# Reordering a normalisation and a rotary turn, and running seven more blocks by a seven-product scheme, in a hybrid encoder layer

## The chip, the cores and the metric

The kernel runs on one core of a Trainium2 chip. The metric is device time in microseconds (us) of one execution. The engines named below are TensorE (PE, matrix products into PSUM, 8 banks), VectorE (DVE), ScalarE (ACT), GpSimd (POOL), and the queues that issue DMAs (SP's, ACT's and POOL's).

## What is computed

One encoder layer for 256 tokens of width 2048, all in float32. Three mixers read the same normed tokens: multi-head latent attention (8 heads, rotary key shared), a gated short convolution, and cross-attention of 4 heads into 256 memory tokens. Three sigmoid gates weigh their projections; then comes an output projection, a convolutional SwiGLU feed-forward block (width 5632) and a last norm.

```python
h = rmsnorm(x, mix_norm)
z = h @ w_in        # [q latent 512 | kv latent 512 | rotary key 64 | conv 3 x 1024 | memory query 1024 | 3 gates x 2048]
q  = (rmsnorm(c_q, q_norm) @ w_uq).reshape(B, S, 8, 128 + 64)     # the last 64 are turned by the rotary angles
kv = (rmsnorm(c_kv, kv_norm) @ w_ukv).reshape(B, S, 8, 128 + 128)
y_mla  = mla_attention(q_nope, q_rope, k_nope, apply_rope(k_r, cos, sin), v) @ w_o_mla
y_conv = (cb * dwconv_centred(cc * cv, conv_w)) @ w_out_conv
y_mem  = memory_attention(q_x, rmsnorm(mem, mem_norm), w_mem_kv) @ w_o_mem
gates  = sigmoid(g + gate_bias)
x = x + (gates[0] * y_mla + gates[1] * y_conv + gates[2] * y_mem) @ w_o
u = dwconv_centred(rmsnorm(x, ffn_norm) @ w_up, ffn_conv_w); a, b = split(u, 2)
x = x + (silu(a) * b) @ w_down
return rmsnorm(x, final_norm)
```

## The kernel before

**Number format.** Every float32 operand is split into a high and a low half, `hi` (a copy by ACT, L146) and `lo` (a difference by DVE, L147), and a product is made of three matmuls (hi·hi, lo·hi, hi·lo). Activations lie side by side as `[hi | lo]` in one tile, 256 + 256 columns. A weight block is 128 x 2048 numbers, 1 MB: SP's queue loads it into one of 3 `raw` buffers, ACT and DVE split it into one of 3 `hi` and one of 3 `lo` buffers, and PE uses it for some 5.5 us.

**Pools.** Activations of 512 columns lie in one pool, `slots`, of 54 buffers: normed tokens `xs` (16), memory tokens `ms` (16), memory keys `kx` (8) and values `vx` (8), latents, memory queries `qx` (8), heads' probabilities and results, gates, and later the feed-forward's tiles. Work tiles of 512 columns (biases, `t`, `sums`) lie in a tag of 4 buffers. Matmul results go to 5 PSUM banks (`mmps`), attention and transposes to 3 (`atps`).

**Order.** The program is written as one straight list; loops are unrolled. When it is built, a scheduler places each engine's instructions in a fixed order, by the place in the program and by when it reckons that operands and buffers are to be had. On the chip every engine works through its list in order and waits on semaphores.

**Stages.** (1) Latents of keys and values, then of queries (not yet normed: `kvz`, `qz`); memory keys; token norms; memory values. (2) L422 to L427: each of the 8 latent tiles is multiplied by its factor `fb` and split into a new slot (`zkv`, `zq`). (3) L430 to L450: the positions are loaded and brought into range on DVE in a chain of some 20 small steps, and ACT makes `sin` and `cos` in the slot `rot`. (4) The rotary key (L559 to L568), then 8 memory query tiles (L572 to L588), each one block of `w_in`, its total (`total`: ACT copies one half of the bank, DVE adds the other) and its split into a slot `qx`. At tile 0 the rotary key is folded, its halves are swapped by four small DMAs (`swapped`), turned (`rope`) and split (`krs`). At every odd tile a memory head is begun; `advance` carries each head in flight by one step: scores and softmax (`p`), transposes (`ph`, `pl`), products with the values (`om`). (5) Convolution blocks alternate with the steps in `STEPS`: rotary queries `r` (four matmul groups, totals into two slots `qr`), keys, values, queries, latent heads 0 to 7. (6) Six gate runs (class `Two`), one for each branch and half of the columns; after each run `gated` makes the sigmoids and two projections follow. (7) Output projection, then twice: 22 `up` steps and the down runs (`Two` again, three in all), with `added` adding their eight products to the residual.

**The seven-product scheme.** A `Two` run multiplies 256 tokens by 1024 columns over 8 (gates) or 11 (down) blocks, each of two 128-row parts. It works on 2 x 2 quarters. `plain` makes 8 quarter products, 24 matmuls of 512 columns. `fast` makes 7, 21 matmuls, but of sums: of the weights (L786 to L788, and a second split, L781 and L782) and of the tokens (`token_sums`, L724 to L736, into two slots `sh`, `sl`). The eight results of a run (`q1` to `q7` and `d`) take all 8 PSUM banks. `GATES` and `FAST` name the blocks that are fast: 6 x 3 in the gate runs and 3 x 4 in the down runs, 30 in all. The gates' token sums are made ahead of all gate runs (`hsums`, L838 to L844), the down runs' within `up`.

Of the kernel before, what the change touches and what calls it, by code (L numbers as in the profile page):

```python
# [11 lines left out]
F32 = mybir.dt.float32  # L12
# [3 lines left out]
ALU = mybir.AluOpType  # L16
# [47 lines left out]
WAKE = 6  # L64
NW = D // 512
KEPT = 10
GATES = (1, 3, 5)
FAST = (1, 3, 5, 7)
STEPS = "r - k0 v0 - q0 0 1 2 3 k1 v1 q1 4 5 - 6 - 7 -"
STEP = 4096.0  # L70
COARSE = _parts(TWO_PI * STEP, 7, 5)
# [7 lines left out]
def tile_kernel(ctx: ExitStack, tc: tile.TileContext, a, out):  # L79
# [3 lines left out]
    raws = ctx.enter_context(tc.tile_pool(name="raws", bufs=3))  # L83
    his = ctx.enter_context(tc.tile_pool(name="his", bufs=3))
    los = ctx.enter_context(tc.tile_pool(name="los", bufs=3))
    slots = ctx.enter_context(tc.tile_pool(name="slots", bufs=54))
    tmp = ctx.enter_context(tc.tile_pool(name="tmp", bufs=2))
    tiny = ctx.enter_context(tc.tile_pool(name="tiny", bufs=2))
    mmps = ctx.enter_context(tc.tile_pool(name="mmps", bufs=5, space=PSUM))
# [5 lines left out]
    def slot(name, dtype=F32):  # L95
        return slots.tile([P, 2 * T], dtype, tag="slot", name=name)

    def half(t, i):
        return t[:, i * T : (i + 1) * T]
# [16 lines left out]
    def col(name, i=0):  # L116
        if name == "fcw":
            return taps[:, i : i + 1]
        c = COLS[name] + i
        return cols[:, c : c + 1]  # L120
# [82 lines left out]
    def split(dst, src, gain=None):  # L203

        w = dst.shape[1] // 2
        if gain is None:
            nc.scalar.activation(dst[:, 0:w], src, AF.Copy)
            nc.vector.tensor_tensor(dst[:, w:], src, f32(dst[:, 0:w]), op=ALU.subtract)
        else:
            nc.scalar.activation(dst[:, 0:w], src, AF.Copy, scale=gain)  # L210
            nc.vector.scalar_tensor_tensor(
                dst[:, w:], src, gain, f32(dst[:, 0:w]), op0=ALU.mult, op1=ALU.subtract
            )
# [23 lines left out]
    def spread(r, dst=None):  # L237

        ps = atps.tile([P, 2 * T], F32, tag="at", name="pss")
        for h in range(2):  # L240
            dg = tmp.tile([P, P], F32, tag="dg", name="dg")
            nc.vector.tensor_scalar(dg, ident, r[:, h : h + 1], None, op0=ALU.mult)
            nc.tensor.matmul(ps[:, h * P : (h + 1) * P], ones, dg, start=True, stop=True)
        if dst is None:
            return ps[:, 0:T]
        nc.scalar.activation(dst, ps[:, 0:T], AF.Copy)
        return dst
# [87 lines left out]
    def token_factor():  # L335

        for rs in row_factor(a["xr"], "x"):
            if rs is None:
                yield
        rsb = spread(rs, const.tile([P, T], F32, name="rsb"))  # L340
        rs2 = const.tile([P, 2], F32, name="rs2")
        nc.vector.tensor_tensor(rs2, rs, rs, op=ALU.mult)
        yield rs, rsb, rs2
# [76 lines left out]
        f = latent_factor(*((kvsq, "kv", 1.0), (qsq, "q", (NOPE + ROPE) ** -0.5))[n])  # L420
        spread(f, half(fb, n))
    zkv, zq = [], []  # L422
    for n, (z, zs, gain) in enumerate(((kvz, zkv, "kvn"), (qz, zq, "qn"))):
        for i in range(4):
            nc.vector.tensor_tensor(z[i], z[i], half(fb, n), op=ALU.mult)
            zs.append(slot(f"z{gain}{i}", F32R))
            split(zs[i], z[i], col(gain, i))  # L427


    pos = half(slot("pos", I32), 0)  # L430
# [21 lines left out]
    def swapped(x, w):  # L452

        sw = slot("sw")
        for q in range(4):
            o = q ^ 1
            nc.scalar.dma_start(
                sw[q * 32 : (q + 1) * 32, 0 : w * T], x[o * 32 : (o + 1) * 32, 0 : w * T]
            )
        return sw  # L460

    def rope(x, sw, w):

        for i in range(w):
            nc.vector.tensor_tensor(half(x, i), half(x, i), cos, op=ALU.mult)
            nc.vector.tensor_tensor(half(sw, i), half(sw, i), sin, op=ALU.mult)
            nc.vector.tensor_tensor(half(x, i), half(x, i), half(sw, i), op=ALU.add)
# [68 lines left out]
    def memory_head(h):  # L536
        vsl = []
        for j in range(2):
            c = slice((h % 2) * T + j * P, (h % 2) * T + (j + 1) * P)
            vsl.append([(vh[:, c], vl[:, c]) for vh, vl in vx[h // 2]])  # L540
        return attend(
            products(qx[2 * h], kx[2 * h]) + products(qx[2 * h + 1], kx[2 * h + 1]), half(mb, 0),
            vsl, f"om{h}_", om,
        )
# [3 lines left out]
    def advance(start=None):  # L548

        for g in list(flying):  # L550
            if next(g, 0) == 0:
                flying.remove(g)
        if start is not None:
            next(start)
            flying.append(start)
# [16 lines left out]
    for i in range(8):  # L572
        qx.append(slot(f"qx{i}", F32R))
        split(qx[i], total(mm(*wblock(), 0, xs)), XD**-0.5)
        if i == 0:
            fold = tmp.tile([P, P], F32, tag="dg", name="fold")
            for h in range(2):
                nc.vector.tensor_tensor(
                    fold[:, 64 * h : 64 * h + 64], ident[:, 0:64], ident[:, 64:], op=ALU.add
                )  # L580
            ps = atps.tile([P, 2 * T], F32, tag="at", name="psk")
            nc.tensor.matmul(ps[:, 0:T], fold, both, start=True, stop=True)
            kr = slot("kr")
            nc.scalar.activation(half(kr, 0), ps[:, 0:T], AF.Copy)
            rope(kr, swapped(kr, 1), 1)
            krs = slot("krs", F32R)
            split(krs, half(kr, 0))
        advance(memory_head(i // 2) if i % 2 == 1 else None)  # L588


# [147 lines left out]
    class Two:  # L738
# [34 lines left out]
        def fast(self, p):  # L773
            raw = next(load(self.src[:, p * WB : (p + 1) * WB]))
            b = [raw[:, i * 512 : (i + 1) * 512] for i in range(4)]

            def two(*parts):
                hi = his.tile([P, WB], F32R, tag="hi", name="hi")
                lo = los.tile([P, WB], F32R, tag="lo", name="lo")
                for s in parts:  # L780
                    nc.scalar.activation(hi[:, s], raw[:, s], AF.Copy)  # L781
                    nc.vector.tensor_tensor(lo[:, s], raw[:, s], f32(hi[:, s]), op=ALU.subtract)  # L782
                return hi, lo

            hi, lo = two(slice(0, 512), slice(1024, 2048))
            nc.vector.tensor_tensor(raw[:, 0:1024], raw[:, 0:1024], raw[:, 512:1536], op=ALU.add)  # L786
            nc.vector.tensor_tensor(b[2], b[0], b[2], op=ALU.add)
            nc.vector.tensor_tensor(b[3], b[2], b[3], op=ALU.add)  # L788
            hi2, lo2 = two(slice(0, 1024), slice(1024, 2048))
            x1, x2_ = self.xs[2 * p : 2 * p + 2]  # L790
            sh, sl = self.sums[p]

            def sums(i):
                return sh[:, (i - 1) * P : i * P], sl[:, (i - 1) * P : i * P]

            self.add("q1", *self.part(x1, 0), hi, lo, 0)
            self.add("q3", *sums(4), hi, lo, 2)
            self.add("q2", *self.part(x2_, 0), hi, lo, 3)
            self.add("q5", *sums(1), hi2, lo2, 0)
            self.add("q7", *sums(3), hi2, lo2, 1)  # L800
            self.add("q6", *sums(2), hi2, lo2, 2)
            self.add("q4", *self.part(x2_, 1), hi2, lo2, 3)
# [32 lines left out]
            pending.pop(0)()  # L835


    hsums = {}  # L838
    for p in GATES:
        t = wide("t")  # L840
        for j in range(2):
            x = f32(xs[2 * p + j])
            nc.vector.tensor_tensor(half(t, j), x[:, 0:T], x[:, T:], op=ALU.add)
        hsums[p] = token_sums(t)  # L844

    def gated(q, g, b1, b2):
        def to(x, y, z, op=ALU.add):
# [16 lines left out]
    for br, w, src in ((2, "wom", om), (1, "woc", yc), (0, "woa", oa)):  # L864
        for jp in range(2):
            bias = [wide("bias") for _ in range(2)]
            for i in range(2):
                o = br * D + (2 * jp + i) * 512
                nc.scalar.dma_start(bias[i], a["gb"][:, o : o + 512])
            q = Two(a["wg"][br * 2 + jp], xs, hsums).run()  # L870
            g = [[slot("g") for i in range(2)] for h in range(2)]
            gated(q, g, *bias)
            for i in range(2):
                n = 2 * jp + i
                bp = project(a[w], n, src, flush)
                for h in range(2):
                    x = g[h][i]
                    nc.vector.tensor_tensor(x, bp[h], x, op=ALU.mult)
                    if br == 2:
                        ms_[h, n] = x  # L880
                    else:
                        nc.vector.tensor_tensor(ms_[h, n], ms_[h, n], x, op=ALU.add)
                if br == 0:
                    mg[4 * n : 4 * n + 4] = [slot(f"mg{i}", F32R) for i in range(4)]
                    pending.append(
                        lambda n=n: turned([ms_[h, n] for h in range(2)], mg[4 * n : 4 * n + 4])
                    )
# [266 lines left out]
```

## Time and profile before

| | |
|---|---|
| median of 3 runs | 1615.64 us (1615.07 to 1615.82) |
| the profiled execution, its own time | 1617.46 us |
| its span, first to last instruction | 1615.7 us |
| PE busy | 1596.3 us (99%), 8228 matmuls |
| DVE busy | 1232.8 us (76%) |
| ACT busy | 837.2 us (52%) |
| mean granted clock of PE | 0.994 |
| from HBM | 314.36 MB, 196 GB/s |

The table is one execution seen by the profiler. Busy time of PE is modelled, so it shows where PE has no work rather than how well it works. The profile's views give starts in us from the span's beginning, and put idle time down to what ended it.

### The profile page before, as it was taken

How to read it: one execution, taken by the hardware profiler on the slowest of the kernel's cores; microseconds unless marked ns; L12 is line 12 of the kernel's file. 1: busy time of each engine (PE TensorE's matmuls, PEld its weight loads, DVE VectorE, ACT ScalarE, POOL GpSimd, SP SyncE). 2: the span in 40 equal slices, each digit the busy share in tenths (PEclk: the TensorE clock that was granted, in tenths of full speed). 3: DMA queues.
4: the chain of work that ended last, by engine and by line, in shares of the span. 5: the costliest groups of instructions: out<-in, count | busy, mean ns of one | idle time of the engine just before them, and what ended most of it. 6: DMA issues, size and time to landing. Idle time of an engine off the chain costs nothing.

```text
span 1615.7 us, 20680 instructions
## 1 busy us (share of the span) xinstructions
PE 1596.3 (99%) x8228; PEld 1370.4 (85%) x8228; DVE 1232.8 (76%) x1574; ACT 837.2 (52%) x1067; POOL 10.5 (1%) x23
## 2 busy tenths in 40 slices
PE   9999989999999999999999999999999999999997
PEld 8888878989888888888888888888888888888886
DVE  6787757776978788788655788888888788888864
ACT  7754546555545445455444555555545555554543
POOL 0000001000000000000000000000000000000000
PEclk9999989999999999999999999999999999999999
DMA  8865534444556466465665455545556555554653
GB/s 318 327 245 192 180 124 169 148 172 157 186 218 248 156 221 245 168 226 187 217 208 195 183 185 195 194 183 183 182 208 227 190 183 185 199 190 157 237 204 106
DMA packets 53152, 318.98 MB, mean 197 GB/s; under 512 B 6208, under 2 KB 7616, under 8 KB 16960
## 3 DMA queue, kind: packets, MB, share of 16 engines
q1 hardware_dynamic: 48528, 310.93, 53.0%
q10 hardware_dynamic: 3888, 6.20, 1.2%
q8 instruction: 65, 1.06, 0.3%
q0 software_dynamic: 640, 0.52, 0.2%
q14 instruction: 31, 0.25, 0.0%
HBM read 314.36 MB, written 2.10 MB: 196 GB/s over the span
## 4 chain that ended last, share of the span: by engine, by line
PE 98%; issue 0%; ACT 0%; DVE 0%; DMA 0%; POOLq 0%; POOL 0%; ACTq 0%
PE ps L174 29%; PE ps L756 26%; PE ps L176 16%; PE ps L700 6%; PE ps L702 6%; PE ps L701 6%; PE ps L178 2%; PE ps L392 1%; PE ps L394 1%; PE ps L393 1%; PE pss L481 1%; PE ps L187 1%; PE ps L191 0%; PE ps L711 0%; PE po L520 0%
## 5 line engine op out<-in xcount | busy, mean ns | idle before, releaser
L147 DVE TENSOR_TENSOR lo<-raw,hi 128x2048 fp32r<-128x2048 f32 (+2 forms) x264 | 575.6, 2182 | 255.8 <-ACT hi L146 255.4
L146 ACT ACTIVATE hi<-raw 128x2048 fp32r<-128x2048 f32 (+2 forms) x264 | 481.3, 1826 | 216.4 <-PE ps L702 70.9
L174 PE MATMUL ps<-h,hi 128*128 128x512 f32 x1845 | 445.4, 392 | 0.0
L174 PEld LDWEIGHTS ps<-h,hi 128*128 128x128 f32 x1845 | 346.8, 189 | 69.5
L176 PEld LDWEIGHTS ps<-h,lo 128*128 128x128 f32 x1968 | 253.5, 191 | 9.6
L176 PE MATMUL ps<-h,lo 128*128 128x256 f32 x1968 | 258.7, 283 | 0.0
L198 ACT ACTIVATE hl<-ps 128x256 f32<-128x256 f32 x149 | 57.1, 384 | 284.6 <-PE ps L178 272.9
L756 PE MATMUL ps<-hi,h 128*128 128x512 f32 x588 | 187.9, 389 | 0.0
L781 ACT ACTIVATE hi<-raw 128x512 fp32r<-128x512 f32 (+1 forms) x120 | 110.3, 948 | 132.1 <-DVE raw L786 72.3
L782 DVE TENSOR_TENSOR lo<-raw,hi 128x512 fp32r<-128x512 f32 (+1 forms) x120 | 128.2, 1088 | 10.1 <-ACT hi L781 9.9
L756 PE MATMUL ps<-hi,f 128*128 128x512 f32 x408 | 129.9, 389 | 0.0
L756 PEld LDWEIGHTS ps<-hi,h 128*128 128x128 f32 x588 | 110.4, 188 | 22.9
L756 PE MATMUL ps<-lo,h 128*128 128x512 f32 x294 | 114.6, 390 | 0.0
L756 PEld LDWEIGHTS ps<-hi,f 128*128 128x128 f32 x408 | 76.6, 188 | 15.8
L756 PE MATMUL ps<-lo,f 128*128 128x512 f32 x204 | 79.4, 389 | 0.0
L200 DVE TENSOR_TENSOR t<-ps,hl 128x256 f32<-128x256 f32 x129 | 54.4, 423 | 26.6 <-ACT hl L198 24.0
L756 PEld LDWEIGHTS ps<-lo,h 128*128 128x128 f32 x294 | 55.2, 188 | 12.1 <-DVE lo L147 0.7
L700 PE MATMUL ps<-hi,mg 128*128 128x512 f32 x128 | 49.7, 392 | 0.0
L701 PE MATMUL ps<-lo,mg 128*128 128x512 f32 x128 | 49.6, 389 | 0.0
L702 PE MATMUL ps<-hi,mg 128*128 128x512 f32 x128 | 49.5, 389 | 0.0
L178 PE MATMUL ps<-h,hi 128*128 128x512 f32 x123 | 48.7, 396 | 0.0
L756 PE MATMUL ps<-lo,sh 128*128 128x512 f32 x120 | 46.7, 389 | 0.0
(298 smaller groups left out, 2062.2 us busy)
## 6 DMA issues: line engine op xcount, KB each, us to landing
raw<-in_wup SPq DMA_DIRECT2D x88, 1024.0 KB, 4.8
raw<-in_wg SPq DMA_DIRECT2D x48, 1024.0 KB, 4.6
raw<-in_win SPq DMA_DIRECT2D x35, 1024.0 KB, 4.8
raw<-in_wd SPq DMA_DIRECT2D x33, 1024.0 KB, 4.6
raw<-in_wo SPq DMA_DIRECT2D x16, 1024.0 KB, 4.8
raw<-in_wdn SPq DMA_DIRECT2D x10, 1024.0 KB, 4.8
raw<-in_wmk SPq DMA_DIRECT2D x8, 1024.0 KB, 5.7
raw<-in_wmv SPq DMA_DIRECT2D x8, 1024.0 KB, 4.9
```

The lines of the kernel that those rows point to most:

```text
L146: nc.scalar.activation(hi[:, s], raw[:, s], AF.Copy)
L147: nc.vector.tensor_tensor(lo[:, s], raw[:, s], f32(hi[:, s]), op=ALU.subtract)
L174: nc.tensor.matmul(ps, hi[:, ks[k]], xs[k], start=first and k == 0, stop=False)
L176: nc.tensor.matmul(ps[:, 0:T], lo[:, ks[k]], xs[k][:, 0:T], start=False, stop=False)
L178: nc.tensor.matmul(ps, hi[:, ks[k]], xs[k], start=False, stop=True)
L198: nc.scalar.activation(hl, ps[:, T:], AF.Copy)
L700: nc.tensor.matmul(ps, xh, hi[:, s], start=first, stop=False)
L701: nc.tensor.matmul(ps, xh, lo[:, s], start=False, stop=False)
L702: nc.tensor.matmul(ps, xl, hi[:, s], start=False, stop=final)
L756: nc.tensor.matmul(self.q[name], x, w[:, s], start=name not in self.begun, stop=self.left[name] == 0,)
L781: nc.scalar.activation(hi[:, s], raw[:, s], AF.Copy)
L782: nc.vector.tensor_tensor(lo[:, s], raw[:, s], f32(hi[:, s]), op=ALU.subtract)
```

## The change

- The eight latents are no longer normed and split in one go before the positions; a function `normed_latent(i)` does one at the end of each memory query tile, the four of the queries first.
- The rotary key is still folded and its halves swapped at tile 0, but turned and split at tile 2.
- Fast blocks: `GATES` (1, 3, 5) becomes (0, 2, 4, 6) and `FAST` (1, 3, 5, 7) becomes (0, 2, 4, 6, 8). The first gate run uses only blocks 2 and 4, so there are 2 + 5 x 4 + 3 x 5 = 37.
- The gates' token sums are made by the first run that uses them: blocks 2 and 4 in the first, 0 and 6 in the second.
- `slots` has 56 buffers, and the tokens' factor `rsb` lies in one of them and no longer in a tile of its own.

```diff
-GATES = (1, 3, 5)
-FAST = (1, 3, 5, 7)
+GATES = (0, 2, 4, 6)
+FAST = (0, 2, 4, 6, 8)
...
-    slots = ctx.enter_context(tc.tile_pool(name="slots", bufs=54))
+    slots = ctx.enter_context(tc.tile_pool(name="slots", bufs=56))
...
-        rsb = spread(rs, const.tile([P, T], F32, name="rsb"))
+        rsb = spread(rs, half(slot("rsb"), 0))
...
-    for n, (z, zs, gain) in enumerate(((kvz, zkv, "kvn"), (qz, zq, "qn"))):
-        for i in range(4):
-            nc.vector.tensor_tensor(z[i], z[i], half(fb, n), op=ALU.mult)
-            zs.append(slot(f"z{gain}{i}", F32R))
-            split(zs[i], z[i], col(gain, i))
+
+    def normed_latent(i):
+        n, z, zs, gain = ((1, qz, zq, "qn"), (0, kvz, zkv, "kvn"))[i // 4]
+        i %= 4
+        nc.vector.tensor_tensor(z[i], z[i], half(fb, n), op=ALU.mult)
+        zs.append(slot(f"z{gain}{i}", F32R))
+        split(zs[i], z[i], col(gain, i))
...
-            rope(kr, swapped(kr, 1), 1)
+            ksw = swapped(kr, 1)
+        if i == 2:
+            rope(kr, ksw, 1)
             krs = slot("krs", F32R)
             split(krs, half(kr, 0))
+        normed_latent(i)
         advance(memory_head(i // 2) if i % 2 == 1 else None)
...
+            if callable(self.sums[p]):
+                self.sums[p] = self.sums[p](p)
             sh, sl = self.sums[p]
...
-    hsums = {}
-    for p in GATES:
+    def own_sums(p):
         t = wide("t")
         for j in range(2):
             x = f32(xs[2 * p + j])
             nc.vector.tensor_tensor(half(t, j), x[:, 0:T], x[:, T:], op=ALU.add)
-        hsums[p] = token_sums(t)
+        return token_sums(t)
+
+    hsums = {}
...
+            for p in GATES[1:3] if br == 2 and jp == 0 else GATES:
+                hsums.setdefault(p, own_sums)
             q = Two(a["wg"][br * 2 + jp], xs, hsums).run()
```

## The prediction

> **What bounds the kernel now.** I read the page first (busy shares, then the 40 slices), then stretches of 10 us where a slice falls short, then the chain that ended last, then the timelines of ScalarE (ACT), VectorE (DVE) and TensorE (PE) around the one hole.
>
> ```profile
> span 1615.7 us, 20680 instructions
> PE 1596.3 (99%) x8228; PEld 1370.4 (85%) x8228; DVE 1232.8 (76%) x1574; ACT 837.2 (52%) x1067; POOL 10.5 (1%) x23
> PE   9999989999999999999999999999999999999997
> ...
> 220.00:230.00 10.00, 6.54 (x39) 5.74 (x38) 5.89 (x12) 4.42 (x9) 0.00 (x0) 0.81 0.41 134
> 230.00:240.00 10.00, 6.69 (x31) 5.96 (x31) 4.36 (x10) 2.39 (x7) 0.00 (x0) 0.67 0.21 83
> 240.00:250.00 10.00, 10.00 (x50) 8.57 (x49) 7.21 (x20) 4.08 (x8) 0.00 (x0) 0.84 0.20 46
> ```
>
> PE is busy but for 19.4 us. Between start and tail there is one hole, 220 to 240 us (in the stretches the columns are length, then PE, PEld, DVE, ACT and POOL busy, granted clock, DMA share, GB/s), and the clock falls with it: 0.81, 0.67, 0.84. So only fewer matmuls or a smaller hole can shorten the run, and only a late DVE or ACT can lengthen it.
>
> ```profile
> 213.11 0.44 PE pst L508 x4
> 216.38 1.44 PE pss L481 x12
> 230.40 2.57 PE pss L481 x12
> 240.07 4.94 PE ps L174 x15
> 252.77 3.42 PE ps L174 x15
> 474.57 41.48 PE ps L756 x183
> 1130.34 114.26 PE ps L756 x504
> ...
> 214.55 0.40 PE L178 MATMUL ps<-zqn,hi 128*128 128x512 f32 x1
> 223.23 0.60 PE L508 MATMUL pst<-ident,p 128*128 128x128 f32 x4
> 225.88 0.39 PE L518 MATMUL po<-ph,vxh 128*128 128x256 f32 x1 [2.05 <-ACT ph L512]
> ```
>
> These are rows of the chain (start, us, what), then three of PE's timeline (in brackets the wait before and what ended it). Each gate run is 183 matmuls (5 plain blocks of 24, 3 seven-product ones of 21), each down run 252 (7 plain, 4 fast), and 114.26/504 = 0.2267 us apiece, with no gap.
>
> *The hole's price.* From 223.23, where the third conv block has been issued, PE does 4 transposes, 12 products, 12 scores, 4 transposes, 12 products (memory heads 2 and 3, L481 to L520) before it takes the next conv block at 240.07. At full clock that is 0.44 + 1.44 + 1.44 + 0.44 + 1.44 = 5.2 us (12 products of 256 columns taken as the 12 scores), so 240.07 - 223.23 - 5.20 = 11.64 us are lost, and 4.94 - 3.42 = 1.52 us on the next block at the lower clock: 13.2 us.
>
> *Why it is there.* Timelines of ACT and DVE:
>
> ```profile
> 148.03 0.69 DVE L399 TENSOR_TENSOR vxl<-ps,vxh 128x512 fp32r<-128x512 f32 x1
> 154.35 0.43 DVE L200 TENSOR_TENSOR t<-ps,hl 128x256 f32<-128x256 f32 x1
> 154.48 0.33 ACTq L431 DMA_DIRECT2D pos<-in_pos  x1
> 158.02 1.67 DVE L211 SCALAR_TENSOR_TENSOR zqn<-z,cols,zqn 128x256 fp32r<-128x256 f32 x4
> 159.60 0.29 DVE L433 CAST ang<-pos 128x256 f32<-128x256 int32 x1
> 174.22 0.42 ACT L448 ACTIVATE rot<-ang 128x256 f32<-128x256 f32 x1
> 174.54 0.40 ACT L210 ACTIVATE qx<-t 128x256 fp32r<-128x256 f32 x1
> 174.85 0.37 ACT L584 ACTIVATE kr<-psk 128x256 f32<-128x256 f32 x1
> 184.33 0.40 ACT L207 ACTIVATE krs<-kr 128x256 fp32r<-128x256 f32 x1
> 184.63 0.41 ACT L210 ACTIVATE qx<-t 128x256 fp32r<-128x256 f32 x1
> 193.55 0.47 ACT L491 ACTIVATE p<-pss,nm 128x256 f32<-128x256 f32 x1 [2.26 <-DVE nm L485]
> 237.12 0.69 DVE L513 TENSOR_TENSOR pl<-pst,ph 128x512 fp32r<-128x512 f32 x1 [1.27 <-ACT ph L512]
> 237.73 0.75 DVE L200 TENSOR_TENSOR qr<-ps,hl 128x256 f32<-128x256 f32 x2
> ```
>
> The first writes of tiles of the pool of slots come strictly in the order of the program: rot, qx0, kr, krs, qx1, p of head 0, ... pl of head 3, qr. qx0's total was there by 154.8 (the t row), yet its split came right behind the sine, and qx1's right behind krs. So I read that a slot is handed out only after every earlier one, and one late link delays all behind it. The last link is the rotary queries: their last matmul group was issued at 214.55, but their totals could not be written before 237.73, so they hold four of the five PSUM banks of that pool, the third conv block the fifth, and PE has nothing else to start. The next block starts right after (240.07).
>
> **The change part by part.**
>
> *Seven more fast blocks.* Gate runs: one of 6 x 24 + 2 x 21 = 186 and five of 180, against six of 183: 12 matmuls fewer. Three down runs of 249 against 252: 9 fewer. 21 x 0.2267 = 4.76 us off PE, on the path.
>
> They cost DVE time. A plain and a fast block in the down stage:
>
> ```profile
> 1148.26 2.29 DVE L147 TENSOR_TENSOR lo<-raw,hi 128x2048 fp32r<-128x2048 f32 x1 [1.17 <-ACT hi L146]
> 1150.47 1.82 DVE L782 TENSOR_TENSOR lo<-raw,hi 128x512 fp32r<-128x512 f32 x2
> 1152.21 1.22 DVE L786 TENSOR_TENSOR raw<-raw 128x1024 f32<-128x1024 f32 x1
> ...
> 1154.80 2.44 DVE L782 TENSOR_TENSOR lo<-raw,hi 128x1024 fp32r<-128x1024 f32 x2
> 1158.46 2.29 DVE L147 TENSOR_TENSOR lo<-raw,hi 128x2048 fp32r<-128x2048 f32 x1 [1.23 <-ACT hi L146]
> 1180.80 1.29 DVE L812 TENSOR_TENSOR x<-x,u 128x512 f32<-128x512 f32 x2
> ...
> 410.80:452.30 41.50, 41.50 (x183) 33.77 (x182) 39.89 (x52) 23.11 (x22) 0.00 (x0) 1.00 0.62 224
> 452.30:474.50 22.20, 22.20 (x100) 18.38 (x99) 15.86 (x16) 10.81 (x10) 0.00 (x0) 1.00 0.59 220
> 474.50:516.00 41.50, 41.50 (x185) 34.37 (x184) 34.75 (x33) 21.22 (x17) 0.00 (x0) 1.00 0.58 207
> 1171.20:1187.50 16.30, 16.30 (x73) 13.51 (x72) 16.01 (x18) 5.42 (x4) 0.00 (x0) 1.00 0.71 262
> ```
>
> The pair takes 10.2 us (24 + 21 matmuls: PE sets it); DVE needs 2.2 for the plain block and 6.8 for the fast one, and waits 1.2. A block turned fast thus adds 4.6 us of DVE and takes 0.68 off PE. A gate run with four: 34.75 + 4.6 = 39.4 us of DVE in 40.8: 97%. The cover is narrow but has held: in the first gate run DVE was busy 39.89 of 41.5 and PE had no gap. ACT stays near half busy. No transfer is added; a fast block holds its raw buffer longer, with the DMA engines at 0.6. Cost in the alternating part: nothing.
>
> The tight place is where two down runs meet (1171.2 to 1187.5: DVE busy 16.01 of 16.3, in the three plain blocks that end a run). There DVE also adds the eight products to the residual. After the change only two plain blocks follow the last fast one, and the next run begins with a fast one. From the end of that last fast block, PE wants the second half of the next fast block after 2 x 5.44 + 9 x 0.2267 = 12.9 us. By then DVE has to do one plain split (2.2), the twelve additions (1.29/2 = 0.65 each, 7.7) and a fast split but for its last 1.1 (5.7): 15.6 at worst, 13.0 if the last four additions wait. So a gap of 0.1 to 2.7 us; I take 1.7, nearer the worst, since the additions come first in the program. Runs that meet `up` or a projection have only plain splits of 2.2 us per 5.44 on one side; I take none there.
>
> How a gap of 1.7 us acts on the clock: the row at 230.40 shows half rate behind a wait of 2.05. If this gap did the same, 1.5 us (4.94 - 3.42) would come on top; I leave that for the range. The Trainium skill, "TensorE: Matmul & The Clock Gate", Part 1, says that the clock halves after an idle window of about 3.4 us and comes back after as much sustained work. By that rule a gap of 1.7 us costs only itself; the row speaks for less patience, and by the row the forecast would be 1.5 us higher.
>
> *Token sums at first use.* Per gate pair two sums, four differences and a split: three times 512 columns at 0.69 us (the pl row), 2.1, and some 0.5 for being cut into seven pieces, an estimate of 2.6 us of DVE. Before, run 1 made three sets; now it makes two, and run 2 the other two. Run 1, the fullest stretch, loses 2.6 us and one fast block's 4.6; run 2 gains 5.2 beside its own fast block. The stretch 452.3 to 474.5 between them had DVE idle for 22.20 - 15.86 = 6.3 us, and the sums need only token tiles that exist. Cost: none; without that cover up to 5.2 us in run 2. One more set of differences in each of the two `up` groups, 1.8 us by the same rate: none, a fast pair sits in some 22 us of `up` matmuls and DVE was 76% busy over the span.
>
> *Latents and rotary key.* The eight normings (per latent a multiply, a copy on ACT and a difference, about 0.42 each, from 1.67/4) leave the stretch 145 to 160 and come back one per memory query tile, behind the tile's split; the rotary queries need the first four, the keys the others. Nothing is removed. What is gained is order. A small DMA of this stretch (the half swaps of qr) lands in 2.0 us:
>
> ```profile
> DMA to landing us min/median/max: 2.0/2.0/2.1
> ```
>
> The positions' slot now follows vxl (148.03 + 0.69) and not zqn: with 0.33 to issue and 2.0 to land the CAST can start near 151.1, not 159.60, 8.5 us sooner, and the sine and qx0 follow, near 166. Then qx1 no longer stands behind krs: kr to krs was 184.33 - 174.85 = 9.5 us. Together p of head 0 comes up to 18.0 us sooner, near 176. krs, now behind qx2, is ready near 166.4 + 9.5 = 176, at the same time, so it should hold up little. For the hole to close, qr must be written before PE is through with the third conv block, 223.2: 14.5 us sooner than 237.73. 18.0 is enough by 3.5; if all the DVE time of the normings (8 x 2 x 0.42 = 6.7 us) fell on that chain, 11.3 would leave 3.2 us of the hole. I take the hole as closed: -13.2; ends: 0 (the chain has another late link that I don't see) and -13.2.
>
> *56 slots, rsb in one of them.* No instruction more; two slots replace one constant. rsb is dead once the tokens are normed, before the stretch in question. Nothing.
>
> **Sum.** Against the profiled execution, 1617.46 us (span 1615.7): -4.76 - 13.2 + 1.7 = -16.3, so 1601.2. The median of the runs is 1615.64, 1.8 below it: 1599.4.
>
> **Rivals.** (1) *The wait moves on.* The hole closes by half, because rope and krs hold the chain behind qx2: for it speaks that both arrive together at 176; against it that every later link has gained as much. 1615.64 - 4.76 + 1.7 - 6.6 = 1606.0. If nothing closes: 1612.6, or 1610.9 without the gap. (2) *DVE becomes the bound, slower.* Every run that now starts fast waits for its split as reckoned for one place: 1.7 + 1.5 = 3.2 us each. For it: DVE at 97% in the runs. Against: the first gate run, 96% with no gap. Two to five such gaps, hole closed: 1604 to 1614. Eight runs start fast (five gate, three down); (4.76 + 13.2)/3.2 = 5.6, so from six gaps on the kernel is slower; at all eight 1597.7 + 25.6 = 1623. (3) *The matmuls fall but PE does not end sooner:* DVE sets the pace of the runs and the -4.76 is eaten; with the hole open that is 1615.6, no change.
>
> **Chances.** Hole closed, at most one gap: 0.58 (1596.5 to 1602.5; 1597.7 without the gap, and about 1 us of reading error). Hole partly open: 0.17 (around 1606). Hole open: 0.08. Two to five gaps: 0.10. Six or more: 0.07. The range 1596.5 to 1611 leaves out some 0.15. What can be told from no change is 0.2%, 3.2 us: faster means under 1612.4. Faster: 0.58 + 0.17 + 0.05 + 0.07 = 0.87; same 0.06; slower 0.07.
>
> **What will show it.** PE busy throughout 220 to 240 with the clock at 1.00, and the rotary queries' totals before 223: step three right. The sine near 166, head 0's exponential near 176. Chain rows of 186 and then 180 matmuls at 0.2267 us (41.8, then 40.8 us), and 249 in 56.4: step one. A PE gap behind DVE near the meeting of the two down runs, some 18 us sooner than 1187: the 1.7. The forecast is wrong if the sine stays near 174, if qr is still last to get its slot after 223, or if PE waits on DVE `lo` at the start of many runs.

## The result and the profile after

The changed kernel takes 1607.22 us (median of four runs, 1606.14 to 1607.86); the kernel before took 1615.73 us beside it. The ratio is 0.9944, with a 95% interval of 0.9931 to 0.9956. The change is faster by 8.5 us. The forecast was 1599.4 us, so about half of the expected gain did not come. The profiled execution took 1607.86 us, its span 1606.0: 9.7 us less span than before.

The page's busy shares and two of the stretches of the hole, in the kernel after (columns as in the prediction):

```profile
PE 1589.5 (99%) x8207; PEld 1363.5 (85%) x8207; DVE 1268.1 (79%) x1633; ACT 850.2 (53%) x1091; POOL 10.5 (1%) x23
...
220.00:230.00 10.00, 8.39 (x56) 7.21 (x54) 6.34 (x8) 4.51 (x9) 0.00 (x0) 0.96 0.44 163
230.00:240.00 10.00, 8.62 (x41) 7.54 (x40) 6.20 (x16) 2.12 (x6) 0.00 (x0) 0.70 0.49 157
```

There are 21 matmuls fewer (8228 to 8207) and 35.3 us more DVE time, about as reckoned (seven blocks at 4.6, sums 2.6 and 3.6: 38). But the hole is still there: PE is idle for 3 of the 20 us from 220 to 240, and the granted clock falls to 0.70.

Where the 9.7 us came from is read from three marks of the chain: the first gate run, the first down run, the end. In the kernel after they read:

```profile
404.04 37.65 PE ps L762 x166
441.92 4.53 PE ps L762 x20
467.98 36.27 PE ps L762 x160
504.48 4.53 PE ps L762 x20
...
1120.60 59.15 PE ps L762 x260
1179.83 2.54 ACT hi L787 x3
```

Up to the first gate run 6.8 us were gained (before, the first gate run began at 410.8, where the prediction's stretch of it starts): that is the hole, where 13.2 was forecast. From there to the first down run 3.0 (1130.34 - 410.8 = 719.5, and 1120.60 - 404.04 = 716.6): the gate runs are now 166 + 20 = 186 and then 160 + 20 = 180 matmuls, with no gap, 12 fewer at 0.2267 being 2.7. From the first down run to the end nothing: the nine matmuls fewer (2.0) are eaten where the two down runs meet. There the chain passes through three copies on ACT (1179.83), which it did not before.

PE's waits in the kernel after (total us, times, longest):

```profile
...
PE ps L762 <- ACT hi L787: 0.8, 1, 0.8
```

This is the meeting of the down runs, and so is one of 0.2 us that is left out. Left out, too, are two that belong to the start and three of one head of the memory attention (head 3), whose probabilities, their split and the split's rest each come late; these three stand in brackets in the next section.

### The profile page after: what moved, and what is told of

Same layout as the page of the kernel before. It is cut to its first block, busy times and chain, and to the rows that moved or that the text cites. A ratio compares the mean times of both kernels' runs of the same rounds, so it can differ in the third digit from the quotient of the medians.

```text
span 1606.0 us, 20737 instructions
## 1 busy us (share of the span) xinstructions
PE 1589.5 (99%) x8207; PEld 1363.5 (85%) x8207; DVE 1268.1 (79%) x1633; ACT 850.2 (53%) x1091; POOL 10.5 (1%) x23
## 4 chain that ended last, share of the span: by engine, by line
PE 98%; ACT 1%; issue 0%; DVE 0%; DMA 0%; POOLq 0%; POOL 0%; ACTq 0%
PE ps L174 29%; PE ps L762 25%; PE ps L176 16%; PE ps L708 6%; PE ps L706 6%; PE ps L707 6%; PE ps L178 2%; PE ps L392 1%; PE ps L394 1%; PE ps L393 1%; PE pss L484 1%; PE ps L187 1%; PE ps L191 0%; PE ps L717 0%; PE pst L511 0%
## 5 line engine op out<-in xcount | busy, mean ns | idle before, releaser
L147 DVE TENSOR_TENSOR lo<-raw,hi 128x2048 fp32r<-128x2048 f32 (+1 forms) x257 | 559.4, 2179 | 206.5 <-ACT hi L146 205.8
L146 ACT ACTIVATE hi<-raw 128x2048 fp32r<-128x2048 f32 (+1 forms) x257 | 467.9, 1823 | 168.5 <-PE ps L708 56.3
L174 PE MATMUL ps<-h,hi 128*128 128x512 f32 x1845 | 445.3, 391 | 0.0
L787 ACT ACTIVATE hi<-raw 128x1024 fp32r<-128x1024 f32 (+1 forms) x148 | 135.5, 948 | 159.3 <-DVE raw L792 102.2
L762 PE MATMUL ps<-hi,h 128*128 128x512 f32 x548 | 177.5, 389 | 0.0
L788 DVE TENSOR_TENSOR lo<-raw,hi 128x1024 fp32r<-128x1024 f32 (+1 forms) x148 | 157.8, 1087 | 6.6 <-ACT hi L787 6.4
L762 PE MATMUL ps<-hi,f 128*128 128x512 f32 x378 | 121.5, 390 | 0.0
L762 PE MATMUL ps<-lo,h 128*128 128x512 f32 x274 | 106.6, 389 | 0.0
L762 PE MATMUL ps<-lo,sh 128*128 128x512 f32 x148 | 57.6, 389 | 0.0
L762 PE MATMUL ps<-hi,sl 128*128 128x512 f32 x148 | 57.1, 389 | 0.0
```

The source lines that it names most:

```text
L174: nc.tensor.matmul(ps, hi[:, ks[k]], xs[k], start=first and k == 0, stop=False)
L762: nc.tensor.matmul(self.q[name], x, w[:, s], start=name not in self.begun, stop=self.left[name] == 0,)
```

## Why the hole closed only half

The links of the chain of slots in the kernel after: DVE's CAST, ACT's sine, the first memory query tile's split, the issue of the rotary key's four swaps, the second tile's split, the exponentials of heads 0, 1 and 3 (each head has two rows, the first is shown), and the rotary queries' first totals. For head 3 the row of before follows.

```profile
148.52 0.28 DVE L436 CAST ang<-pos 128x256 f32<-128x256 int32 x1
168.54 0.42 ACT L451 ACTIVATE rot<-ang 128x256 f32<-128x256 f32 x1
168.87 0.40 ACT L210 ACTIVATE qx<-t 128x256 fp32r<-128x256 f32 x1
169.57 2.71 ACTq L460 DMA_DIRECT2D sw<-kr  x4
172.74 0.41 ACT L210 ACTIVATE qx<-t 128x256 fp32r<-128x256 f32 x1
181.16 0.48 ACT L494 ACTIVATE p<-pss,nm 128x256 f32<-128x256 f32 x1
196.60 0.47 ACT L494 ACTIVATE p<-pss,nm 128x256 f32<-128x256 f32 x1 [1.78 <-DVE nm L488]
...
225.54 0.48 ACT L494 ACTIVATE p<-pss,nm 128x256 f32<-128x256 f32 x1 [1.78 <-DVE nm L488]
231.35 0.75 DVE L200 TENSOR_TENSOR qr<-ps,hl 128x256 f32<-128x256 f32 x2
```

```profile
233.72 0.47 ACT L491 ACTIVATE p<-pss,nm 128x256 f32<-128x256 f32 x1 [2.90 <-DVE nm L485]
```

The CAST came 11.1 us sooner than before (159.60), more than the 8.5 forecast, but the sine only 5.7 (174.22). Between the two lie 20.0 us instead of 14.6, because the angle steps now share DVE with the multiplies of the first latents (1.4 us), with four block splits instead of three (2.3 us more) and with some smaller steps. The groups of DVE from 148.5 to 168.6, in the kernel after:

```profile
L147 DVE TENSOR_TENSOR lo<-raw,hi 128x2048 fp32r<-128x2048 f32 x4 | 9.2, 2292 | 1.4 <-ACT hi L146 1.3
...
L427 DVE TENSOR_TENSOR z<-z,fb 128x256 f32<-128x256 f32 x4 | 1.4, 420 | 0.0
```

The second memory query tile's split came 11.9 us sooner (184.63), where 18.0 was reckoned. It no longer stands behind the turned key, but it stands behind the issue of the key's four swaps: ACT issues them from 169.57 on, for 2.71 us, and starts nothing else meanwhile. Head 0's exponential came 12.4 us sooner (193.55), not 18. Of the 5.6 us that are missing, 2.8 were lost at the sine and 3.3 between the two splits; 0.5 came back behind them.

From head to head the gain then shrank: 8.2 us at head 3, 6.4 at the rotary queries' totals (237.73). Heads 1 to 3 now follow one another in 14.5 us ((225.54 - 196.60)/2), and the whole stretch from head 0 to head 3 took 40.2 us before and takes 44.4 now. PE has no wait from head 0 to the scores of head 3. So work that comes sooner meets a PE that is still busy with its own order: between the scores of two heads it has some 11 us of other matmuls to do, a memory query tile's at first, then those of the convolution blocks and of the rotary queries.

PE at the hole, in the kernel after:

```profile
217.96 3.58 PE L174 MATMUL ps<-h,hi 128*128 128x512 f32 x15
227.34 0.94 PE L511 MATMUL pst<-ident,p 128*128 128x128 f32 x4 [0.77 <-DVE p L503]
229.05 0.42 PE L521 MATMUL po<-ph,vxh 128*128 128x256 f32 x1 [0.77 <-ACT ph L515]
231.49 0.58 PE L523 MATMUL po<-pl,vxh 128*128 128x256 f32 x1 [1.38 <-DVE pl L516]
233.37 4.88 PE L174 MATMUL ps<-h,hi 128*128 128x512 f32 x15
```

Head 3's transposes wait for an exponential that ended after 226, the third conv block is through by then, and no other block can start because the rotary queries hold its banks. So PE stands in head 3's own chain until 233.37, and the next block then runs at the lower clock (4.88 us for 15 matmuls that took 3.58). The granted clock there, in three stretches (the last number but two):

```profile
228.00:229.00 1.00, 0.28 (x3) 0.04 (x1) 0.46 (x1) 1.00 (x2) 0.00 (x0) 1.00 0.00 0
229.30:236.00 6.70, 5.32 (x19) 4.45 (x19) 3.98 (x7) 1.04 (x3) 0.00 (x0) 0.50 0.55 194
236.10:240.00 3.90, 3.90 (x27) 3.51 (x25) 2.92 (x9) 1.08 (x3) 0.00 (x0) 1.00 0.29 68
```

It fell behind the two waits of 0.77 us, between which PE had only four transposes; the wait of 1.38 came after the fall.

## The experiments

Each is the changed kernel with the edit shown.

**Only the order, and only the blocks.** Does the split of the gain hold? The first kernel has the old block sets and all token sums at the start, the second the old place of the normings and of the key's turn.

```diff
-GATES = (0, 2, 4, 6)
-FAST = (0, 2, 4, 6, 8)
+GATES = (1, 3, 5)
+FAST = (1, 3, 5, 7)
...
-    hsums = {}
+    hsums = {p: own_sums(p) for p in GATES}
...
-            for p in GATES[1:3] if br == 2 and jp == 0 else GATES:
-                hsums.setdefault(p, own_sums)
```

> The changed kernel with the old 30 fast blocks and token sums made ahead; normings, rotary turn, 56 slots and rsb as changed. Theory (the hole at the rotary queries was halved by the new order, and the seven extra blocks are a separate gain on PE): the hole costs 6.5 us as in the changed kernel, not 13.2, so 1615.7 - 6.7 = 1609.0, down runs of 252 matmuls without a gap where they meet. Rival (the hole moved because of the blocks or the later token sums): hole of 13.2, 1615.7.

```diff
-    def normed_latent(i):
...
+    for n, (z, zs, gain) in enumerate(((kvz, zkv, "kvn"), (qz, zq, "qn"))):
+        for i in range(4):
+            nc.vector.tensor_tensor(z[i], z[i], half(fb, n), op=ALU.mult)
...
-            ksw = swapped(kr, 1)
-        if i == 2:
-            rope(kr, ksw, 1)
+            rope(kr, swapped(kr, 1), 1)
...
-        normed_latent(i)
```

> The changed kernel with latents normed in one go and the rotary key turned at tile 0 as before; 37 fast blocks, 56 slots, sums at first use. Theory: PE falls by 21 x 0.2267 = 4.76 us and 2.0 us come back in the gap where the two down runs meet; the hole is the old 13.2. 1615.7 - 4.76 + 2.0 = 1612.9. Rival (two more slots alone relieve the hole): under 1610. Rival (DVE bound in many runs): above 1614.

Measured: the order alone 1610.56 us (ratio 0.9964, 0.995 to 0.9978), the blocks alone 1613.63 (0.9982, 0.9973 to 0.9992); before 1616.34. They gain 5.8 and 2.7 us, and the two together 8.5: the parts add up. The hole belongs to the order alone: from 220 to 240 PE is busy 17.1 us with the order alone (17.0 with both) and 13.3 with the blocks alone (13.2 before).

**The normings without the key's turn, and the turn without the normings.** Which of the two moves shortens the chain?

```diff
-            ksw = swapped(kr, 1)
-        if i == 2:
-            rope(kr, ksw, 1)
+            rope(kr, swapped(kr, 1), 1)
```

> The changed kernel with one part of the reorder undone: the latents are still normed one per memory query tile, but the rotary key is turned at tile 0, as before, not behind tile 2. The blocks and token sums stay as changed. Theory (each late link in the order of the slots counts): the positions' cast stays early, near 148.5, and the sine near 168.5, but the second memory query tile's split stands behind the turned key's again, some 9.5 us behind the key's first slot, so head 0's exponential comes near 187 (181.2 with both moved, 193.6 before); the hole closes by about a third to a half of what both moves closed: 1609 to 1611.5 us. Rival (the earlier cast alone carries the gain, and the turned key costs the chain nothing): 1607.2 us, head 0 near 181. Other rival (the key's turn alone carried it): 1614 us, head 0 near 193.

The other kernel takes back the normings alone (the rest of the diff above).

> The changed kernel with the other part of the reorder undone: the latents are normed in one stretch ahead of the positions again, the rotary key is still turned behind memory query tile 2. Blocks and token sums stay as changed. Theory (each late link in the order of the slots counts): the positions' cast is back near 159.6 and the sine near 174, but the second memory query tile's split follows the key's slot within 4 us; head 0's exponential near 186 (186.1 with the normings moved alone, 181.2 with both, 193.6 before), the rotary queries' totals near 231.5, the time as with the normings moved alone, 1608.5 to 1609.5 us. Rival (the earlier cast alone carries the gain of the reorder): head 0 near 193, 1613.5 us.

The exponentials of head 0 and head 3, normings alone first, the key's turn alone second:

```profile
186.06 0.47 ACT L494 ACTIVATE p<-pss,nm 128x256 f32<-128x256 f32 x1 [2.29 <-DVE nm L488]
...
227.26 0.47 ACT L494 ACTIVATE p<-pss,nm 128x256 f32<-128x256 f32 x1 [2.74 <-DVE nm L488]
```

```profile
186.25 0.48 ACT L493 ACTIVATE p<-pss,nm 128x256 f32<-128x256 f32 x1
...
228.78 0.47 ACT L493 ACTIVATE p<-pss,nm 128x256 f32<-128x256 f32 x1 [3.08 <-DVE nm L487]
```

Head 0 comes within 1 us of what was expected in both, so either move by itself takes some 7.4 us out of the chain; together they take 12.4, less than twice as much. Times: 1609.21 and 1608.61 us (ratios 0.9956 and 0.9952, intervals 0.9942 to 0.997 and 0.9937 to 0.9967). Against the blocks alone (1613.63) each move by itself gives 4.4 to 5.0, and both together 6.4. The theory's head times were right; its time for the first kernel, 1609 to 1611.5, was met only at its edge, since the second move adds just 1.4 to 2.0 us.

**The rotary queries out of the chain of slots.** Are their banks what leaves PE without work? Their tile is taken from the rotating pool `wide` instead.

```diff
-            q = slot("qr")
+            q = wide("qr")
```

> The changed kernel with the totals of the rotary queries written into two work tiles of their own and no longer into slots, so that they need not wait until every earlier slot (head 3's pl) is handed out. Theory (the four totals hold PSUM banks while they wait for a slot, and that is why PE has nothing to start): PE takes the next conv block right after the third, no hole between 220 and 240, clock 1.00, 1607.2 - 6.5 = 1600.7, heads 2 and 3 no earlier than in the changed kernel. Rival (PE is held by memory head 3's chain, which stands ahead in its order): the hole stays, 1607.

Measured 1606.84 us (0.9942, 0.9927 to 0.9956): as the rival had it, but not for the rival's reason. PE, DVE and then ACT with its queue in this kernel:

```profile
225.71 3.58 PE L174 MATMUL ps<-h,hi 128*128 128x512 f32 x15
242.77 6.30 PE L174 MATMUL ps<-h,hi 128*128 128x512 f32 x15 [3.86 <-DVE cv L615]
```

```profile
216.39 0.75 DVE L200 TENSOR_TENSOR qr<-ps,hl 128x256 f32<-128x256 f32 x2
...
237.94 0.42 DVE L468 TENSOR_TENSOR qr<-qr,rot 128x256 f32<-128x256 f32 x1 [5.53 <-DMA sw<-qr]
...
242.29 0.42 DVE L615 TENSOR_TENSOR cv<-ps,cv 128x256 f32<-128x256 f32 x1
```

```profile
231.09 6.18 ACTq L460 DMA_DIRECT2D sw<-qr  x8
237.31 0.66 ACT L207 ACTIVATE om<-po 128x256 fp32r<-128x256 f32 x2 [5.63 <-DMA sw<-qr]
```

The first totals are written at 216, and the next conv block starts at 225.71 with no wait: at that place the bank theory is right. But the tiles for the half swaps still come behind head 3 in the chain of slots, so all eight swap transfers are issued at once from 231.09, DVE stands 5.53 us at the turn that needs them, and the conv total (242.29), which is queued behind the turn on DVE, keeps the next block waiting: 3.86 us, and 6.30 instead of 3.42 to 3.58 for the 15 matmuls after it. About 6.7 us come back in another place. So it is the place in the pool that holds the totals back. Whether they are held on the chip, or by the order that the scheduler gave each engine when it reckoned with the pool, the runs don't separate.

**The angles earlier.** If only the chain's length counts, its longest link should move: positions, angles, sine and cosine are made ahead of the token norms, the memory values and the latents' normings.

```diff
+    pos = half(slot("pos", ...
+    ...  (the angles, the sine and the cosine)
     for n in range(2):
         for p in range(4 * n, 4 * n + 4):
             normed(p)
...
-    pos = half(slot("pos", ...
-    ...
     def swapped(...
```

> The changed kernel with the positions' chain and the sine and cosine (L430 to L450 of the kernel before) moved ahead of the memory values; all else as changed. Theory (slots are handed out strictly in program order, and the late slot of the sine holds all memory query slots): the split of query tile 0 comes within some 2 us of its total, near 155 and not 169, head 0's exponential near 168 and not 181, all heads some 12 us sooner, and the hole closes: 1600.7. If the chain's DVE work (some 7 us) lands in the stretch before 145 where DVE is 50 to 60% busy, nothing is lost there; if it does cost, up to 3 us. Rival (query tile 0 waits for something else, such as ACT's order): the split stays near 169, 1607.

```profile
154.47 0.40 ACT L210 ACTIVATE qx<-t 128x256 fp32r<-128x256 f32 x1
...
174.54 0.47 ACT L494 ACTIVATE p<-pss,nm 128x256 f32<-128x256 f32 x1
...
218.31 0.47 ACT L494 ACTIVATE p<-pss,nm 128x256 f32<-128x256 f32 x1 [1.78 <-DVE nm L488]
226.22 0.75 DVE L200 TENSOR_TENSOR qr<-ps,hl 128x256 f32<-128x256 f32 x2
...
230.00:240.00 10.00, 10.00 (x61) 8.84 (x60) 8.02 (x21) 5.46 (x10) 0.00 (x0) 1.00 0.43 139
```

Measured 1600.91 us (0.9905, 0.989 to 0.992): the theory's time. The first memory query split follows its total at once (154.47), head 0 comes at 174.54 (168 was expected), head 3 at 218.31 (7.2 sooner; 12 was expected), and PE is busy throughout with the clock at 1.00. The heads still follow in about 14.5 us each; they only start soon enough.

**The angles alone.** Are the change's own two moves needed then? Here the normings stand in one stretch and the key is turned at tile 0, both as before the change; the angles are early and the blocks as changed.

> The changed kernel's blocks and token sums with the latents normed in one stretch and the rotary key turned at tile 0, both as before the change; the only move left is that the angles are made ahead of the normings (the move that took the changed kernel to 1600.9 us). Theory (only the chain of slots counts, and the angles are its longest link): the first memory query tile's split comes right behind the last normed latent, near 160, the second some 10 us later behind the turned key, head 0's exponential near 179; the heads then follow in 44 us as they did before the change, the rotary queries' totals come near 222.5, the hole is closed: 1601.5 us. Rival (the moves of the normings and of the key are needed too): the hole stays half open, 1606 to 1607 us.

```profile
167.79 0.41 ACT L210 ACTIVATE qx<-t 128x256 fp32r<-128x256 f32 x1
176.71 0.47 ACT L493 ACTIVATE p<-pss,nm 128x256 f32<-128x256 f32 x1 [2.19 <-DVE nm L487]
...
219.42 0.48 ACT L493 ACTIVATE p<-pss,nm 128x256 f32<-128x256 f32 x1 [1.78 <-DVE nm L487]
227.09 0.74 DVE L200 TENSOR_TENSOR qr<-ps,hl 128x256 f32<-128x256 f32 x2
```

Measured 1600.86 us (0.99, 0.9883 to 0.9916). The hole is closed without either move: in this kernel the change's reorder is worth nothing measurable once the angles are early (1600.86 against 1600.91). One expectation missed: the totals came at 227.09 and not near 222.5, and the hole closed all the same. What goes with the time is head 3's exponential: at 218.31 and 219.42 its transposes fit into the tail of the third conv block (which ends at 226 to 227), at 225.54 and later they do not. That fits the six kernels that have the changed blocks and differ only in these moves (219.4 and below: about 1601 us; 225.5: 1607; 227 to 229: 1609; 233.6, with the blocks alone: 1613.6); where between 219.4 and 225.5 it tips was not tried. It is not a cause by itself: with the totals in work tiles head 3's exponential came at 225.32, and PE had no wait at this place.

**The meeting of the two down runs.** Three theories: DVE has too little time between two fast blocks that only two plain blocks part (the prediction's), the fast block at the head of a run waits for banks, or DVE is too full throughout. The first kernel has the fast blocks at odd places, the second takes the second down run's blocks in another order, with no matmul more.

```diff
-FAST = (0, 2, 4, 6, 8)
+FAST = (1, 3, 5, 7, 9)
```

> The changed kernel with the five fast blocks of a down run at 1, 3, 5, 7, 9 instead of 0, 2, 4, 6, 8: as many matmuls, but a run now begins with a plain block and ends with one plain block behind its last fast one. Theory (the prediction's reckoning): between the last fast block of one down run and the next fast one of the other there are still two plain blocks (10 and 0), so DVE has the same additions, one plain split and one fast split to do in the same 12.9 us, and the 2.05 us lost at the meeting stay: 1607.2 us, 118.3 us for the 513 matmuls of the two runs. Rival (it is the fast block at the very head of a run that waits, because its products need banks that the additions hold): with a plain block at the head the loss goes, 116.3 us for the two runs, 1605.2 us in all.

```diff
-            q = Two(a["wd2"][g * NW // 2 + n // 2], fs, sums).run()
+            order = (1, 0, 3, 2, 5, 4, 7, 6, 9, 8, 10) if n else None
+            q = Two(a["wd2"][g * NW // 2 + n // 2], fs, sums).run(order)
```

> The changed kernel with only the second down run of the first group taking its blocks in the order 1, 0, 3, 2, 5, 4, 7, 6, 9, 8, 10: three plain blocks (9, 10, 1) lie between the last fast block of the first run and the first fast one of the second, as many as before the change, and no matmul is added. Theory (DVE is late with the second half of a fast block because only two plain blocks give it time for the twelve additions): PE waits no more at the meeting, the two runs take 116.3 instead of 118.35 us, 1605.2 us in all. Rival (the loss is spread over the runs because DVE is too full, whatever the order): 118 us again, 1607.2 us.

The stretch 1170 to 1200 of the kernel after, then of the odd places, then of the other order:

```profile
1170.00:1200.00 30.00, 29.06 (x125) 23.06 (x125) 28.11 (x32) 12.66 (x12) 0.00 (x0) 1.00 0.48 176
```

```profile
1170.00:1200.00 30.00, 28.91 (x126) 23.29 (x125) 28.77 (x32) 13.11 (x13) 0.00 (x0) 1.00 0.53 191
```

```profile
1170.00:1200.00 30.00, 30.00 (x134) 24.81 (x133) 26.87 (x29) 12.38 (x12) 0.00 (x0) 1.00 0.50 187
```

With a plain block at the head but still only two between the fast ones, PE is idle for 1.1 us of the 30, as in the kernel after (0.9); with three between, for none. What ends the wait differs. With the odd places it is one of the additions, which frees the bank that a plain block's products need:

```profile
PE ps L762 <- DVE x L820: 1.0, 1, 1.0
```

In the kernel after it is the last of ACT's three copies of 1179.83, which belong to the fast block at the head and to the next one. One of them needs the head block's last weight sum, and DVE made that only at 1179.49, behind additions:

```profile
1179.49 0.69 DVE L794 TENSOR_TENSOR raw<-raw 128x512 f32<-128x512 f32 x1
```

Times: 1606.68 us (0.9939, 0.9926 to 0.9951) and 1605.13 us (0.9934, 0.9921 to 0.9948). The two times alone lie too close to tell; the traces do. Chain rows of the kernel after (a block of the next stage), then of the other order (the two down runs, and the same block):

```profile
1252.23 3.42 PE ps L174 x15
```

```profile
1119.36 108.60 PE ps L762 x478
...
1249.18 3.42 PE ps L174 x15
```

In the other order the chain stays on PE for 478 matmuls (0.2272 us apiece), and from the first down run's start to that block it takes 129.8 us, against 131.6 (1252.23 - 1120.60): 1.8 us shorter. So it is the distance between fast blocks that costs, and its price is 1.8 us, not the 2.05 that I had read from the runs' length. The bank theory is wrong in that a plain block at the head does not help; but a bank that an addition holds is what PE waits for in one of the two kernels. DVE is busy for 28.1 and 28.8 of the 30 us where PE waits, and for 26.9 where it does not.

**Both remedies together.** The early angles and the other order.

> The changed kernel with the angles of the rotary turn made ahead of the latents' normings (as in the run that measured 1600.9 us) and with the order of the second down run as in the kernel that puts a plain block first there. Theory: both gains stand in different places and add up: 1600.9 - 2.05 = 1598.9 us, ratio to before 0.989. Rival for the meeting (loss spread over the runs): 1600.9 us.

Measured 1599.69 us (1599.16 to 1599.79; ratio 0.9896, 0.9883 to 0.991), against 1598.9 expected. That is 5.4 us under the kernel with the other order and 1.2 under the one with early angles, less than the 1.8 of the traces; the intervals are too wide to tell 1.2 from 1.8. PE's list of waits holds nothing but the start:

```profile
PE ps L184 <- ACT h L210: 1.8, 1, 1.8
PE ps L277 <- POOL ident masks.py:199: 1.5, 1, 1.5
```

## Why the prediction was right or wrong

- *Seven more fast blocks, -4.76:* right. The gate runs gave 3.0 for 2.7, the down runs' 2.0 is there but covered by the gap; the blocks alone measured 2.7 (4.76 less 1.8 is 3.0). One figure was a slip: 186 x 0.2267 is 42.2 and not 41.8, and the chain shows 42.2 (37.65 + 4.53).
- *DVE's cover:* right. 35 us more on DVE and no gap in any gate run, with the token sums moved into them; the third rival and the slower one fell.
- *The gap where two down runs meet, 1.7:* right in place and size (1.8), and in that the distance between fast blocks makes it. Of the mechanism a part was missing: DVE's additions do stand between the steps of the fast split, but the wait ends with the last of three copies on ACT, and ACT was not in the reckoning.
- *The clock behind such a gap:* the 1.5 us on top did not come; 1170 to 1200 shows 1.00 with a longest wait of 0.76. At the hole the clock fell to 0.50 behind two waits of 0.77 us within 2.5 us. The rule that the prediction took from the Trainium skill, "TensorE: Matmul & The Clock Gate", Part 1, asks for an idle window of about 3.4 us. It fits the lone gap and not the hole, where no wait was longer than 1.38. For the hole, the section on psum-queue depth-cycling of that page of the Trainium skill agrees: it tells of short idle times between groups of matmuls that are frequent enough to throttle the clock.
- *The hole closes, -13.2:* this term was mis-sized; -6.8 came. The step that failed reads "p of head 0 comes up to 18.0 us sooner, near 176. [...] 18.0 is enough by 3.5". The chain's order and its last link were read rightly (each of the two moves by itself takes some 7.4 us out of it, and the totals released early close that place), but the gain was 12.4 us at head 0. The angle steps took 20.0 us beside the normings instead of 14.6, and the second query tile's split stood behind the key's four swaps on ACT (2.71 us), which the prediction put at nothing. One reading was wrong in the other direction: the positions' slot does not follow `vxl`. Their DMA was issued at 143.37, before the last `vxl` (147.91), and took 4.0 us to land where 2.0 was reckoned; so the CAST came 2.6 us sooner than the 151.1 of the forecast. And the first rival's "against", that every later link gains as much, was wrong: PE's fixed order between the heads let 6.4 us through to the rotary queries. That rival, with a chance of 0.17, is what came. Its price, 1606.0, was right within 1.3 us, but by luck: a hole half closed was an assumption. It had named the turned key as its cause; but the key was split right behind the third query tile (182.38 after 182.07), and the runs show the angles.
- *The criterion:* by the prediction's own sign ("if qr is still last to get its slot after 223") this step failed, at 231.35. As a limit, "qr must be written before [...] 223.2" was too strict. The hole closed with the totals at 226 and 227, because head 3's work fills PE until then if its exponential is early.

## What to carry to other kernels

When tiles of one pool are handed out in program order, look for the longest link of that order and start it where its inputs first exist; here that one move did more (12.8 us beside the blocks) than the two moves that shortened the links around it (6.4), and made them needless. A gain at the head of a chain does not arrive whole at its end: follow it through the engine whose order is fixed and ask at the last link whether it is still enough. Releasing one resource early shifts the wait to the next one held in the same chain, so list everything that the late step allocates (here the totals and the swaps).

## What the hardware showed that was not expected

Issuing small transfers holds ACT. In the kernel with the totals in work tiles, eight issued back to back kept ACT's queue busy for 6.18 us (seven of about 0.6 each, one of 1.44), and ACT's next instruction (the copy of `om`, 237.31) began only behind them. In the kernel after they went out in two groups of four, 2.44 us each. So transfers that cost little one at a time are a stall when a late slot releases them together.

The granted clock fell from 1.00 to 0.50 behind two waits of 0.77 us with four transposes between them, and not behind a lone wait of 0.76 or, with the fast blocks at odd places, of 0.96. Whether the transposes or the number of waits made the difference, the runs don't show. Once it had fallen, it stayed at 0.50 for 6.8 us: 229.3 to 236.1 in the kernel after, 226.1 to 233.0 and again 236.3 to 243.2 in the kernel before, and 241.5 to 248.4 in the kernel with the totals in work tiles, where the wait was 3.86 us. So in these traces short waits that brought the clock down cost as long a stretch at half rate as a long one.
